# The first chunk of x in two token halves on two queues, all its transposes ahead of the first product

## The chip, the cores and the metric

The kernel runs on one core of one Trainium2 chip. The metric is the device time of one execution in microseconds, from the launch to the end of the last engine; the median of several runs is given. Profiles are of one execution, and their times count from the first instruction that the profiler shows. TensorE (PE in the profile) multiplies, VectorE (DVE), ScalarE (ACT) and GpSimd (POOL) do the elementwise work, and SyncE (SP) mostly starts transfers; ScalarE and GpSimd can start transfers too.

## The reference

One layer of an encoder: a root-mean-square norm of x, one wide input projection, two groups of heads side by side (attention, and a gated linear recurrence, the LRU), and one output projection that is added to x.

```python
def hybrid_layer(x, norm_w, w_in, ...):
    h = rms_norm(x, norm_w)
    proj = jnp.einsum('bsd,de->bse', h, w_in)
    q, k, v, g_attn, xr, g_lru = jnp.split(proj, SPLITS, axis=-1)
    attn_out = attention_group(q, k, v, q_norm_w, k_norm_w)
    lru_out = lru_group(xr, conv_w, conv_b, ...)
    mixed = jnp.concatenate([rms_norm(attn_out, attn_norm_w) * jax.nn.silu(g_attn),
                             rms_norm(lru_out, lru_norm_w) * jax.nn.silu(g_lru)], axis=-1)
    return x + jnp.einsum('bse,ed->bsd', mixed, w_out)
```

x has 512 tokens by 2048 columns, w_in 2048 by 4608, w_out 2048 by 2048, all in float32. Only the start of the input projection matters for this change.

## The kernel before

**The products.** Each float32 operand is split into a high part, rounded to a type that TensorE takes in one pass (`fp32r` in the profile), and the low rest; a product is the sum of three, high by high, high by low and low by high. The first projection is `proj_feat(C_XR, a1, first, given)`: it has the LRU's input features on the partitions and all 512 tokens as the moving operand, four accumulators of 128 by 512 (`pj`), and it walks over the 2048 columns of x in eight chunks of 256 (`c`), each of two halves of 128 (`kk`). For the first two chunks (line 394) the products go in six groups of four per chunk: high weight by high x, low weight by high x, high weight by low x, first for one half, then for the other. Between the groups the generator yields, and the caller does other work there (`move`, lines 1206 to 1221): loads and transposes of later chunks of x, splits of later weights.

**x.** `xload` (line 239) loads one chunk of x as 4 tiles of 128 tokens by 256 columns (`b` in the profile) on SyncE's queue, in `nk` pieces by columns. `xturn` (line 254) turns one half of it so that the columns lie on the partitions: four transposes on TensorE (line 258), one per token tile, into one bank of PSUM. ScalarE then multiplies by the norm's weights and rounds (line 263), which makes the high part, and VectorE makes the low part (line 266). The division by the root mean square comes later, on the results. `columns` (line 190) turns the norm's weights themselves by one small transpose (line 194).

**Weights.** `wraw` (line 205) loads 256 rows by 512 columns of `w_in` on SyncE's queue, here in two pieces of 128 rows, and `wsplit` (line 216) splits one such piece: a copy that rounds (line 223; on VectorE for the first chunk), and a subtraction on VectorE (line 224).

**The start.** TensorE's instructions run in the order of the program text. It begins with `WARM` = 12 fillers (`busy`, line 1165: bf16 products of a tile of ones with itself into a bank that nobody reads), which need the tile `ones` that VectorE writes at line 159. Then come lines 1178 to 1192: the loads are started in the order first half of x's chunk by columns, first weight piece, second half of x, second weight piece, all by SyncE, with the norm's weights by ScalarE. ScalarE loads its function table with a one-column Exp. TensorE turns the norm's weights, turns the first half of x (`xturn(xc, 0, split_first)`, where `split_first` puts the first weight piece's split ahead of x's scaling), and does `WARM2` = 5 more fillers. The first group of four products follows (`proj_feat` then yields `None`), and at line 1224 the second weight piece is split, the second half of x is turned and scaled, and the next chunk's loads are started.

Later chunks of x below `TURNED` = 5 go through `xchunk` and `xturn` too; the last three are turned by VectorE and a trip through device memory instead (`blocks`, `put_aside`, `bring_back`).

Of the kernel before, what the change touches and what calls it, by code (L numbers as in the profile page):

```python
# [17 lines left out]
P = 128  # L18
# [3 lines left out]
NT = SEQ // P  # L22
# [17 lines left out]
SOON = 150  # L40


WARM, WARM2 = 12, 5


BEGIN, STEPS, LATE = 11, 2, 3
# [10 lines left out]
C_Q, C_K, C_GA, C_XR, C_GL = 0, 1024, 1536, 2560, 3584  # L57
# [6 lines left out]
def hybrid_kernel(  # L64
# [20 lines left out]
    nc = tc.nc  # L85
    xf = x.rearrange("b s d -> (b s) d")
# [31 lines left out]
    def nm(s):  # L118
        cnt[0] += 1
        return f"{s}_{cnt[0]}"  # L120

    def x2():
        return pools["xw"].tile([P, SEQ], F32R, tag="x2", bufs=32, name=nm("x2"))
# [4 lines left out]
    def b4(dt=F32, shape=(P, 2, SEQ)):  # L128
        return pools["lru"].tile(list(shape), dt, tag="b4", bufs=LRU_B4, name=nm("b4"))
# [13 lines left out]
    def mm():  # L143
        return ps.tile([P, SEQ], F32, tag="mm", name=nm("mm"))

    def const(shape, name, dt=F32):
        return cp.tile(list(shape), dt, tag=name, name=name)

    def f(ap):
        return ap.bitcast(F32)  # L150
# [7 lines left out]
    ones = const([P, P], "ones")  # L158
# [46 lines left out]
    def wraw(w, r0, c0, nk=1, queue=nc.sync):  # L205

        raw = wring.tile([P, 2, SEQ], F32, name=nm("wr"))
        src = w[r0 : r0 + 2 * P, c0 : c0 + SEQ].rearrange("(k p) e -> p k e", p=P)
        for k in range(nk):
            ks = slice(k * 2 // nk, (k + 1) * 2 // nk)  # L210
            loads_done[queue] = queue.dma_start(raw[:, ks, :], src[:, ks, :]).ins
            yield raw
# [3 lines left out]
    def wsplit(raw, k, copy=nc.scalar.copy):  # L216

        turn_of[0] += k
        pool = pools["wx" if "wx" in pools and turn_of[0] % 2 else "xw"]
        hi = pool.tile([P, SEQ], F32R, tag="wh", bufs=4, name=nm("wh"))  # L220
        lo = pool.tile([P, SEQ], F32R, tag="wl", bufs=4, name=nm("wl"))
        done = (
            copy(hi, raw[:, k, :]).ins,  # L223
            nc.vector.tensor_sub(lo, raw[:, k, :], f(hi)).ins,  # L224
        )
        split_done[-1] = split_done[turn_of[0] - k] = done
        return hi, lo
# [8 lines left out]
    ssq = const([P, NT, KT // 2], "ssq")  # L236
    highs, x_parts, squared = {}, [], []

    def xload(c, nk=1):

        xc = b4(shape=(P, NT, 2 * P))
        for k in range(nk):
            ks = slice(k * 2 * P // nk, (k + 1) * 2 * P // nk)
            cs = slice(c * 2 * P + ks.start, c * 2 * P + ks.stop)
            nc.sync.dma_start(xc[:, :, ks], xf[:, cs].rearrange("(t p) d -> p t d", p=P))
            yield xc

    def behind(those):
        stack = ExitStack()
        for ins in those:  # L250
            stack.enter_context(tc.issue_after(ins))
        return stack

    def xturn(xc, kk, then=None):
        pt = mm()
        for t in range(NT):
            ks = slice(kk % 2 * P, (kk % 2 + 1) * P)
            nc.tensor.transpose(pt[:, t * P : (t + 1) * P], xc[:, t, ks], ident)  # L258
        if then:
            then()  # L260
        xh[kk], xl[kk] = x2(), x2()
        with behind(split_done[-1] if kk > 3 else ()):
            highs[kk // 2] = nc.scalar.activation(
                xh[kk], pt, AF.Identity, scale=nw[:, kk : kk + 1]
            ).ins
        nc.vector.scalar_tensor_tensor(
            xl[kk], pt, nw[:, kk : kk + 1], f(xh[kk]), op0=ALU.mult, op1=ALU.subtract
        )

    def xsquare(xc, c):  # L270
        for t in range(NT):
            if c >= TURNED:
                nc.scalar.activation(
                    xc[:, t, :], xc[:, t, :], AF.Square, accum_out=ssq[:, t, c : c + 1]
                )
                continue
            square = nc.vector.scalar_tensor_tensor(
                xc[:, t, :], xc[:, t, :], 1.0, xc[:, t, :], op0=ALU.mult, op1=ALU.mult,
                accum_out=ssq[:, t, c : c + 1],
            )  # L280
            if c == 1:
                squared.append(square.ins)

    def blocks(u, t, src):

        nc.vector.transpose(
            u[:, :, :, t, :].rearrange("p b k r -> p k b r"),
            src.rearrange("p (k b c) -> p k b c", k=2, c=B),
        )

    def put_aside(u, tag, bufs):

        aside_ = dram.tile([P, NQ, 2 * SEQ // NQ], F32, name=nm(tag), tag=tag, bufs=bufs)
        nc.sync.dma_start(aside_, u.rearrange("p b k t r -> p b (k t r)"))
        return aside_
# [9 lines left out]
    def in_order(v):  # L305
        return v.rearrange("p (t i r) -> p i t r", t=NT, i=NQ)

    def xchunk(c):
        with tc.high_priority(AHEAD):
            (xc,) = xload(c)  # L310
        yield
        if c < TURNED:
            with tc.high_priority(AHEAD):
                for k in range(2):
                    xturn(xc, 2 * c + k)
            if c == 2:
                yield
            with behind(split_done[2][1:] if c == 2 else ()):
                xsquare(xc, c)
            yield  # L320
            return
        u, back = (
            ring.tile([P, NQ, 2, NT, B], F32, name=nm("xu")) for ring in (aring, hring)
        )
        with tc.high_priority(AHEAD), tc.issue_after(squared[-1] if c == TURNED else split_done[3][1]):
            for t in range(NT):
                blocks(u, t, xc[:, t, :])
        yield
        with tc.high_priority(AHEAD):
            there = put_aside(u, "xd", KT // 2 - TURNED)  # L330
        with tc.issue_after(highs[TURNED - 1]):
            xsquare(xc, c)
        yield
        with tc.high_priority(AHEAD):
            bring_back(back, there)
        yield
        with tc.high_priority(AHEAD), behind(split_done[-1]):
            for k in range(2):
                kk = 2 * c + k
                xh[kk], xl[kk] = x2(), x2()  # L340
                hi, lo = (in_order(v) for v in (xh[kk], xl[kk]))
                v = back[:, :, k]
                nc.scalar.activation(v, v, AF.Identity, scale=nw[:, kk : kk + 1])
                x_parts[:] = nc.scalar.copy(hi, v).ins, nc.vector.tensor_sub(lo, v, f(hi)).ins
        yield
# [31 lines left out]
    def xstats():  # L377
        s = const([P, NT], "xsum")
        nc.vector.reduce_sum(s, ssq, axis=AX.X)
        rsqrt_mean(rstd, s, DM, NT)  # L380
        yield from rows(rbc, rstd, lambda: k2(F32R, (P, NT, P)))
# [778 lines left out]
    ctx.enter_context(tc.manual_schedule(engines={mybir.EngineType.PE}))  # L1160

    a1, a2, a3, a4, a5 = [], [], [], [], []
    warm, wv = mm(), ones.bitcast(mybir.dt.bfloat16)

    def busy(n):
        for _ in range(n):
            nc.tensor.matmul(warm[:, : 2 * P], wv[:, :P], wv, start=True, stop=True)  # L1167
# [8 lines left out]
    )  # L1176
    given = {}
    with tc.high_priority():
        xs, ws = xload(0, 2), wraw(w_in, 0, C_XR, 2)
        nc.scalar.dma_start(nw_st, norm_w.rearrange("(k p) -> k p", p=P))  # L1180
        xc, raw = next(xs), next(ws)
        next(xs), next(ws)
        table = const([P, 1], "table")
        nc.scalar.activation(table, ones[:, :1], AF.Exp)
        first = []

        def split_first():
            first.append(wsplit(raw, 0, nc.vector.tensor_copy))

        columns(nw, nw_st)  # L1190
        xturn(xc, 0, split_first)
        busy(WARM2)
    stats = xstats()
    chunks = [xchunk(c) for c in range(1, KT // 2)]

    raws = {}
# [26 lines left out]
    for step in proj_feat(C_XR, a1, first, given):  # L1223
        if step is None:
            with tc.high_priority():
                first.append(wsplit(raw, 1, nc.vector.tensor_copy))
                xturn(xc, 1)
            xsquare(xc, 0)
            move(None)
            given[1] = wload(w_in, 2 * P, C_XR)  # L1230
            continue
        c, e = step
        move(step)
        if (c, e) == (1, 2):
            s2.close()
        if (c, e) == (4, 2):
            with tc.high_priority(AHEAD):
                vec_load()
        if (c, e) == (7, 1):
            columns(vec, vec_st)  # L1240
        if (c, e) in ((4, 3), (KT // 2 - 1, 0)):
            with tc.high_priority(AHEAD), tc.issue_after(split_done[-1][1]):
                next(stats)
# [216 lines left out]
```

## Time and profile before

| what | value |
|---|---|
| median of 3 runs | 626.5 us (626.13, 626.61, 626.5) |
| the profiled execution | 626.48 us, of which its span is 624.7 us |
| TensorE busy | 620.0 us of the span |
| VectorE, ScalarE, GpSimd busy | 495.3, 352.4, 101.8 us |
| x's first two transfers, 256 KB each | 2.9 us from issue to landing |

In the rows below, the first two numbers of the chain and of the timeline are the start and the duration in microseconds, then come the engine, the line, the operation, the tiles written and read, and how many instructions the row merges. A bracket tells how long the engine was idle before and what released it. "PEld" is TensorE's weight load, and "SPq" and "ACTq" mark instructions that only start a transfer. In the chain a row begins where the row before it ended, so its times can differ by some tenths from the timeline's, where pipelined instructions overlap.

### The profile page before, as it was taken

To read this page: it belongs to the slowest core of one execution; us is meant where nothing else is said; L and a number is where in the kernel's file an instruction comes from. 1 tells how busy PE (TensorE), PEld (TensorE's weight loads), DVE (VectorE), ACT (ScalarE), POOL (GpSimd) and SP (SyncE) were. 2 spreads that over 40 slices of the span, in tenths; PEclk is the share of its full clock that TensorE was granted. 3 is DMA by queue.
4 is the path that set the end of the run, shared out by engine and by line. 5 is a ranking of instruction groups with operands and counts; after the bars stand their busy time and mean duration, and the time that the engine had idled before them with its cause. 6 is when DMAs were issued, how large, how long until landed. Compare 5 with 4: busy or idle time off the path is not lost.

```text
span 624.7 us, 8293 instructions
## 1 busy us (share of the span) xinstructions
PE 620.0 (99%) x2756; PEld 512.6 (82%) x2756; DVE 495.3 (79%) x800; ACT 352.4 (56%) x617; POOL 101.8 (16%) x135
## 2 busy tenths in 40 slices
PE   9999999999999999999999999999999999999997
PEld 7888888888888888888888888888888888888886
DVE  5958979986699876887887888549979866887776
ACT  3675799479946833545485548338345633443441
POOL 0000210112003622622123223100210101010010
PEclk9999999999999999999999999999999999999999
DMA  8878686759774599479659646932995777897252
GB/s 285 277 210 271 178 202 171 175 135 195 239 235 137 170 247 240 100 204 270 192 173 258 201 137 192 256 91 76 283 254 184 216 250 242 288 333 230 68 202 101
DMA packets 74026, 127.61 MB, mean 204 GB/s; under 512 B 6664, under 2 KB 29312, under 8 KB 73984
## 3 DMA queue, kind: packets, MB, share of 16 engines
q1 hardware_dynamic: 66096, 109.65, 56.7%
q0 software_dynamic: 7712, 17.31, 14.3%
q8 instruction: 21, 0.34, 0.2%
q14 instruction: 21, 0.17, 0.1%
q10 hardware_dynamic: 176, 0.14, 0.1%
HBM read 110.29 MB, written 37.75 MB: 237 GB/s over the span
## 4 chain that ended last, share of the span: by engine, by line
PE 99%; DVE 0%; issue 0%
PE pj L154 20%; PE pj L155 20%; PE pj L153 20%; PE mm L1040 14%; PE pj L1040 11%; PE mm L155 4%; PE mm L154 3%; PE mm L153 3%; PE pj L394 2%; PE mm L258 1%; PE mm L1167 1%; PE mm L836 0%; DVE cb L1069 0%; PE mm L194 0%; PE mm L373 0%; DVE ones L159 0%
## 5 line engine op out<-in xcount | busy, mean ns | idle before, releaser
L153 PE MATMUL pj<-x,wh 128*128 128x512 f32 x368 | 143.5, 390 | 0.0
L155 PE MATMUL pj<-x,wl 128*128 128x512 f32 x368 | 143.2, 389 | 0.0
L154 PE MATMUL pj<-x,wh 128*128 128x512 f32 x368 | 143.2, 389 | 0.0
L223 ACT CAST wh<-wr 128x512 fp32r<-128x512 f32 x142 | 84.5, 618 | 81.5 <-PE pj L154 29.8
L224 DVE TENSOR_TENSOR wl<-wr,wh 128x512 fp32r<-128x512 f32 x144 | 98.5, 712 | 20.5 <-ACT wh L223 19.2
L888 ACT CAST wh<-wr 128x1024 fp32r<-128x1024 f32 (+1 forms) x72 | 60.6, 860 | 75.3 <-PE mm L1040 36.0
L889 DVE TENSOR_TENSOR wl<-wr,wh 128x1024 fp32r<-128x1024 f32 (+1 forms) x72 | 68.6, 983 | 29.0 <-ACT wh L888 28.9
L153 PEld LDWEIGHTS pj<-x,wh 128*128 128x128 f32 x368 | 69.1, 188 | 14.4
L154 PEld LDWEIGHTS pj<-x,wh 128*128 128x128 f32 x368 | 69.1, 188 | 14.3
L155 PEld LDWEIGHTS pj<-x,wl 128*128 128x128 f32 x368 | 69.1, 188 | 14.3
L154 PE MATMUL pj<-wl,x 128*128 128x512 f32 x192 | 74.7, 389 | 0.0
L155 PE MATMUL pj<-wh,x 128*128 128x512 f32 x192 | 74.7, 389 | 0.0
L153 PE MATMUL pj<-wh,x 128*128 128x512 f32 x192 | 74.7, 389 | 0.0
L912 POOL DMA_DIRECT2D t<-in_w_out_dram x40 | 33.6, 907 | 156.0 <-DMA t<-in_w_out_dram 96.9
L1040 PE MATMUL mm<-wh,ml 128*128 128x512 f32 x126 | 49.0, 389 | 0.0
L1040 PE MATMUL mm<-wh,mh 128*128 128x512 f32 x126 | 49.0, 389 | 0.0
L1040 PE MATMUL mm<-wl,mh 128*128 128x512 f32 x126 | 49.0, 389 | 0.0
L153 PEld LDWEIGHTS pj<-wh,x 128*128 128x128 f32 x192 | 36.0, 188 | 7.6
L154 PEld LDWEIGHTS pj<-wl,x 128*128 128x128 f32 x192 | 36.0, 188 | 7.5
L155 PEld LDWEIGHTS pj<-wh,x 128*128 128x128 f32 x192 | 36.0, 188 | 7.4
L712 POOL TENSOR_SCALAR p<-p,sm 128x512 f32<-128x512 f32 x32 | 24.2, 761 | 89.4 <-DVE sm L711 89.4
L1040 PE MATMUL pj<-wl,mh 128*128 128x512 f32 (+1 forms) x100 | 38.5, 385 | 0.0
(205 smaller groups left out, 1052.9 us busy)
## 6 DMA issues: line engine op xcount, KB each, us to landing
wr<-in_w_in_dram SPq DMA_DIRECT2D x71, 512.0 KB, 5.0
wr<-in_w_out_dram SPq DMA_DIRECT2D x21, 512.0 KB, 5.1
t<-in_w_out_dram POOLq DMA_DIRECT2D x40, 256.0 KB, 7.1
wr<-t SPq DMA_DIRECT2D x40, 256.0 KB, 5.8
pd<-u SPq DMA_DIRECT2D x16, 512.0 KB, 3.0
pt<-pd SPq DMA_DIRECT2D x64, 128.0 KB, 4.1
t<-in_w_out_dram SPq DMA_DIRECT2D x24, 256.0 KB, 5.3
wr<-in_w_out_dram SPq DMA_DIRECT2D x22, 256.0 KB, 4.2
```

The source lines that it names most:

```text
L153: nc.tensor.matmul(acc, lh, rh, start=start, stop=False)
L154: nc.tensor.matmul(acc, lh, rl, start=False, stop=False)
L155: nc.tensor.matmul(acc, ll, rh, start=False, stop=stop)
L223: copy(hi, raw[:, k, :]).ins,
L224: nc.vector.tensor_sub(lo, raw[:, k, :], f(hi)).ins,
L258: nc.tensor.transpose(pt[:, t * P : (t + 1) * P], xc[:, t, ks], ident)
L394: nc.tensor.matmul(acc[e], w[:, e * P : (e + 1) * P], x_[2 * c + k], start=c == k == j == 0, stop=False,)
L712: last_pool[0] = nc.gpsimd.tensor_scalar(p, p, sm, 0.0, op0=ALU.mult, op1=ALU.add).ins
L888: nc.scalar.copy(hi[:, to], b)
L889: nc.vector.tensor_sub(lo[:, to], b, f(hi[:, to]))
L912: nc.gpsimd.dma_start(dst, src, accum_op=ALU.add)
L1040: nc.tensor.matmul(dst[s][:, es], lh[:, ts_], rh[:, es], start=i == ends_[0] and j == 0, stop=i == ends_[1] and j == 2,)
```

## The change

The first chunk of x is still loaded in two pieces, but by tokens: token tiles 0 and 1 by SyncE, token tiles 2 and 3 by ScalarE, each with all 256 columns. So SyncE's order becomes half of x, first weight piece, second weight piece, and ScalarE's the norm's weights, half of x, table load. `xturn` is taken apart into `xturns`, the transposes, and `xscale`, the scaling and the split. Both halves of the chunk's columns, eight transposes, are turned ahead of the first product; the second half's scaling stays where its turn was, at line 1228 of the old text. Between the transposes and the first product one filler is left of five. The fillers multiply a bf16 constant of ones that the framework's preamble writes, in place of the tile `ones`.

```diff
-WARM, WARM2 = 12, 5
+WARM, WARM2 = 12, 1
...
-    def xload(c, nk=1):
+    def xload(c, queues=(nc.sync,)):
         xc = b4(shape=(P, NT, 2 * P))
-        for k in range(nk):
-            ks = slice(k * 2 * P // nk, (k + 1) * 2 * P // nk)
-            cs = slice(c * 2 * P + ks.start, c * 2 * P + ks.stop)
-            nc.sync.dma_start(xc[:, :, ks], xf[:, cs].rearrange("(t p) d -> p t d", p=P))
-            yield xc
+        n = NT // len(queues)
+        src = xf[:, c * 2 * P : (c + 1) * 2 * P].rearrange("(t p) d -> p t d", p=P)
+        for k, queue in enumerate(queues):
+            ts_ = slice(k * n, (k + 1) * n)
+            queue.dma_start(xc[:, ts_], src[:, ts_])
+        return xc
...
-    def xturn(xc, kk, then=None):
+    def xturns(xc, kk):
         pt = mm()
         for t in range(NT):
             ks = slice(kk % 2 * P, (kk % 2 + 1) * P)
             nc.tensor.transpose(pt[:, t * P : (t + 1) * P], xc[:, t, ks], ident)
-        if then:
-            then()
+        return pt
+
+    def xturn(xc, kk):
+        xscale(xturns(xc, kk), kk)
+
+    def xscale(pt, kk):
         xh[kk], xl[kk] = x2(), x2()
...
-    warm, wv = mm(), ones.bitcast(mybir.dt.bfloat16)
+    warm, wv = mm(), nc.const_aps.tensor(1.0, [P, 2 * P], mybir.dt.bfloat16)
...
-        xs, ws = xload(0, 2), wraw(w_in, 0, C_XR, 2)
         nc.scalar.dma_start(nw_st, norm_w.rearrange("(k p) -> k p", p=P))
-        xc, raw = next(xs), next(ws)
-        next(xs), next(ws)
+        xc, ws = xload(0, (nc.sync, nc.scalar)), wraw(w_in, 0, C_XR, 2)
+        raw = next(ws)
+        next(ws)
...
-        def split_first():
-            first.append(wsplit(raw, 0, nc.vector.tensor_copy))
-
         columns(nw, nw_st)
-        xturn(xc, 0, split_first)
+        pts_ = [xturns(xc, k) for k in range(2)]
         busy(WARM2)
+        first.append(wsplit(raw, 0, nc.vector.tensor_copy))
+        xscale(pts_[0], 0)
...
-                xturn(xc, 1)
+                xscale(pts_[1], 1)
```

More of the change, by code (lines that the diff above doesn't have):

```diff
@@ L309, in xchunk @@
         with tc.high_priority(AHEAD):
-            (xc,) = xload(c)
+            xc = xload(c)
         yield
```

## The prediction

> **What bounds the kernel now.** I read the page first (busy shares and the chain that ended last), then the chain for the first 24 us, then the timeline of that stretch, because the diff touches nothing behind it, and last the transfers and the windows there.
>
> ```profile
> PE 620.0 (99%) x2756; PEld 512.6 (82%) x2756; DVE 495.3 (79%) x800; ACT 352.4 (56%) x617; POOL 101.8 (16%) x135
> PE 99%; DVE 0%; issue 0%
> ```
>
> ```profile
> 1.04 2.74 PE mm L1167 x12
> 3.78 0.21 PE mm L194
> 4.00 1.04 PE mm L258 x4
> 5.04 1.07 PE mm L1167 x5
> 6.11 1.22 PE pj L394 x4
> 7.33 0.44 PE mm L258 x4
> 7.77 3.23 PE pj L394 x14
> 10.99 0.87 PE mm L258 x8
> 11.87 4.13 PE pj L394 x18
> ```
>
> TensorE carries 99% of the chain, so the end moves by what TensorE gains before it becomes dense, and by nothing else. It is dense from 6.11 us on: products of 128x512 follow each other every 0.231 us (3.23 us for 14) and transposes of 128x128 every 0.11 us (0.44 us for 4). Up to 6.11 us it does twelve fillers, the norm weights' transpose (L194), four transposes of x's first 128 columns (L258) and five fillers. The same four transposes took 1.04 us at 4.00 us and 0.44 us at 7.33 us, so the clock was slow at first, by a factor of about two. The first four products took 1.22 us instead of 4 x 0.231 = 0.92 us: 0.30 us lost, which is about 1.3 products at half speed, so the clock turned fast near 6.7 us.
>
> ```profile
> 0.31 0.09 POOL L1445 MEMSET const-bfloat16-1.0<- 128x1 bf16 x1
> 0.72 0.45 ACTq L1180 DMA_DIRECT2D nw_st<-in_norm_w_dram  x1
> ...
> 0.72 0.43 SPq L245 DMA_DIRECT2D b<-in_x_dram  x1
> 0.82 0.17 DVE L159 MEMSET ones<- 128x128 f32 x1 [0.82 <-PEq L1445]
> ...
> 1.20 1.28 ACT L1184 ACT_TABLE_LOAD   x1 [1.20 <-PEq L1445]
> 1.21 0.49 SPq L211 DMA_DIRECT2D wr<-in_w_in_dram  x1
> ...
> 1.74 0.43 SPq L245 DMA_DIRECT2D b<-in_x_dram  x1
> ...
> 2.22 0.51 SPq L211 DMA_DIRECT2D wr<-in_w_in_dram  x1
> ...
> 4.99 0.43 DVE L223 CAST wh<-wr 128x512 fp32r<-128x512 f32 x1 [0.78 <-DMA wr<-in_w_in_dram]
> 5.08 0.69 ACT L263 ACTIVATE x<-mm,nw 128x512 fp32r<-128x512 f32 x1 [2.38 <-PE mm L258]
> ...
> 5.82 1.09 PEld L394 LDWEIGHTS pj<-x,wh 128*128 128x128 f32 x4 [0.19 <-ACT x L263]
> ```
>
> The first product is issued at 5.82 us, released by ScalarE's scaled copy of x (5.08 to 5.77 us), itself released by the four transposes that end at 5.04 us. The weight half's rounding ended earlier, at 4.99 + 0.43 = 5.42 us. So the first link is: x's half landed, four slow transposes, one ScalarE pass of 0.69 us; the five fillers (1.07 us) only cover that pass.
>
> **The change, part by part.** *When x lands.* Before, SP issued x's first 128 columns, a weight half, x's other columns, the other weight half. Now SP issues the first two token tiles, then both weight halves, and ScalarE issues the last two token tiles behind the norm weights. The last two tiles go out at 0.72 + 0.45, about 1.2 us, and the table load (1.28 us) slides from 1.20 to about 1.65 us and ends by 2.95 us, with its small activation of 0.2 us behind it. Nothing on ScalarE is needed before 4.8 us, so that issue is free; it would cost its 0.45 us only if x came 1.7 us earlier than I reckon.
>
> ```profile
> b<-in_x_dram SPq DMA_DIRECT2D x2, 256.0 KB, 2.9
> wr<-in_w_in_dram SPq DMA_DIRECT2D x2, 256.0 KB, 4.4
> ```
>
> ```profile
> 1.00:2.00 1.00, 0.96 (x5) 0.71 (x6) 0.00 (x0) 0.80 (x1) 0.89 (x6) 1.00 0.09 24
> 2.00:3.00 1.00, 1.00 (x7) 0.69 (x6) 0.00 (x0) 0.69 (x2) 0.14 (x1) 1.00 0.92 255
> 3.00:4.00 1.00, 1.00 (x6) 0.49 (x5) 0.00 (x0) 0.00 (x0) 0.00 (x0) 1.00 0.88 294
> 4.00:5.00 1.00, 1.00 (x5) 0.92 (x6) 0.18 (x2) 0.00 (x0) 0.00 (x0) 1.00 0.96 301
> ```
>
> Half of x took 2.9 us from issue to landing, so SP's two tiles land near 0.72 + 2.9 = 3.6 us. No row has a large load on ScalarE's queue, so I bound its landing. By the half of x ahead of all others it is 1.2 + 2.9 = 4.1 us; by the weight halves behind others it is 1.2 + 4.4 = 5.6 us. The bytes give a second pair: by the windows' last column, GB/s, the engines had moved 0.28 MB by 3.0, 0.57 MB by 4.0 and 0.87 MB by 5.0 us; all of x is 0.52 MB, reached at 3.85 us if no weights get between, and x with one weight half is 0.79 MB, reached at 4.7 us. Both tiles and first weight half will share the engines; I take **4.2 us**, near the row of the same size, and keep 3.85 and 5.6 us for the range. Rows of x in one transfer become 1 KB instead of 512 B; I count no gain for it, which errs to the slow side.
>
> The Trainium skill, page "DMA: Bandwidth & Descriptors", section "Issuing engines are not separate DMA queues", says that transfers started from several engines run on the same 16 DMA engines and that only issue time is saved. By that rule alone the second queue brings x no bandwidth, and its landing would go by the bytes (3.85 to 4.7 us here), so the sum stands; the windows, with the engines 88 to 96% busy from 2 us on, agree with it.
>
> *TensorE up to the first product.* The fillers read a constant that GpSimd writes at 0.31 us in the preamble, instead of `ones` (0.82 + 0.17 us). TensorE can start at 0.72 to 0.8 us, when the other engines do, not at 1.04 us: the twelve fillers end near 3.5 instead of 3.78 us. The norm weights follow (0.21 us, to 3.7 us), then two transposes on SP's tiles (2 x 0.26 us at the slow rate of 1.04 us for 4, to 4.2 us), then the two on ScalarE's tiles: 4.2 + 0.52 = 4.72 us. ScalarE's pass runs from about 4.76 to 5.45 us. Under it TensorE does the four transposes of the second 128 columns (1.04 us, to 5.76 us) and the one filler left (1.07 / 5 = 0.21 us), to **5.97 us** against 6.11. So the cover that five fillers gave comes from work that was due anyway, and the bound of the first product passes from ScalarE to TensorE by a few tenths. The weight half must be rounded by then: it is second on SP as before, was rounded by 5.42 us, and even 1.21 + 4.4 + 0.43 = 6.04 us would be only 0.07 us late.
>
> *TensorE behind it.* The four transposes at 7.33 us go: **0.44 us** off the dense part. Of the start, 0.14 us earlier lies in the slow clock and is worth half, 0.07 us. The slow share of the first products is 0.30 us; starting the fillers about 0.3 us earlier can bring between nothing and all of that. Would the clock follow them exactly, 0.32 us less of half speed would be 0.16 us; nothing shows that it does, so I take the middle, 0.08 us. Sum: 0.44 + 0.07 + 0.08 = **0.6 us**.
>
> *What is late next.* VectorE's passes keep their order, weight half, low part, x's low part; they were idle-waiting on the second weight half, which now has 256 KB less ahead of it on SP. The next stops are these:
>
> ```profile
> 10.46 1.15 ACT L223 CAST wh<-wr 128x512 fp32r<-128x512 f32 x2 [1.97 <-DMA wr<-in_w_in_dram]
> ...
> 11.52 1.25 ACT L263 ACTIVATE x<-mm,nw 128x512 fp32r<-128x512 f32 x2
> ...
> 16.32 1.43 DVE L286 STREAM_TRANSPOSE xu<-b 128x256 f32<-128x256 f32 x4 [1.22 <-DMA b<-in_x_dram]
> ...
> 18.96 2.49 DVE L224 TENSOR_TENSOR wl<-wr,wh 128x512 fp32r<-128x512 f32 x4
> ```
>
> ```profile
> 20.75 0.23 PE pj L154
> 20.98 0.24 PE pj L155
> ```
>
> The second chunk's weights land at 10.46 us and ScalarE waits for them before it scales that chunk's x: ready at 11.52 + 0.62 = 12.1 us. TensorE wants it after the eight transposes and six products of the first chunk, 11.87 + 6 x 0.23 = 13.2 us. The margin of 1.1 us takes a gain of 0.6 us even if the landing doesn't move. VectorE's low part for the third chunk, behind x's landing at 16.3 us, is ready at 18.96 + 0.62 = 19.6 us and is wanted at 20.98 us: 1.4 us of margin. SP's later loads are issued one slot sooner (x's fourth transfer at 2.2 us rather than 2.78), which can only widen these. No other row of the chain leaves TensorE, so the 0.6 us should reach the end.
>
> The sum is made on the profiled execution, 626.48 us with a span of 624.7 us; the 1.8 us around the span are untouched. It is 0.02 us below the median of the three runs, 626.5 us, so the forecast is 626.48 - 0.6 = **625.9 us**. A difference under 0.2%, 1.25 us, can't be told from no change by a measurement of this kernel.
>
> **The rivals.** *The clock starts over (slower).* The clock turned fast near 6.7 us, 5.66 us after the first filler. Before, nothing but 1.04 us of transposes stood between two runs of fillers. Now 0.21 + 8 x 0.26 = 2.3 us of transposes and one filler stand there, and if ScalarE's half lands after 4.2 us TensorE is quiet for the difference. If the clock's count starts over at 4.2 us, it turns at 9.86 us: products from 5.97 us run at half speed for 3.89 us and lose 1.95 us, which is 1.65 us more than the 0.30 of now; less the 0.51 us won, 1.1 us slower, **627.6 us**. If it starts over only with the first product, the loss is 5.66 / 2 = 2.83 us and the time 626.48 + 2.53 - 0.51 = 628.5 us. It decides against the change if more than about 1 us of slow products is added, that is if the turn comes after 8.2 us. For it: the fillers exist for some reason and four of five go. Against it: before, the clock turned although transposes filled 1.25 us of the time between 3.78 and 5.04 us.
>
> The Trainium skill, page "TensorE: Matmul & The Clock Gate", Part 4 (PE-mode transpose), states that transposes don't count as TensorE activity for that gate; its Part 1 has the gate looking at free-running windows of about 3.4 us. By that rule the quiet would run from 3.5 us to the filler, and a turn before 8.2 us would need a window that the first fillers fill alone. The trace has too few transposes to settle it.
>
> *ScalarE's half is late, or the gain is eaten (no change).* At 4.7 us the product's start becomes 4.7 + 0.52 + 1.04 + 0.21 = 6.47 us, 0.36 us later than now, against 0.44 us won: 626.4 us. At 5.6 us it is 7.37 us, and 1.26 - 0.44 = 0.8 us are lost: 627.3 us. For it: the weight rows at 4.4 us, and three transfers at once. Against it: both queues now begin with x, and only the first weight half can come beside it.
>
> *An earlier clock (faster).* An earlier x alone gives nothing, since in my sum TensorE works without a pause from its first filler to the first product. But if the earlier fillers let the clock turn by about 4.8 us, the second four transposes take 0.44 instead of 1.04 us and the filler some 0.1 us, so that TensorE is done by 5.3 us and the first product waits for ScalarE alone, until 5.5 us: 0.6 us earlier than 6.11, all of it at the fast rate, with the 0.30 us of slow products and the 0.44 us on top. That is 1.35 us, **625.1 us**. Against it: the fillers begin 0.3 us earlier, and the clock would have to turn 1.9 us earlier. For it: the three runs lie 0.5 us apart, which a turn that isn't tied to the program would give.
>
> **How the numbers follow.** Forecast, 625.5 to 626.2 us: 53%. Late half or eaten gain, 626.2 to 627.3 us: 24%. Clock starts over, 627.2 to 628.5 us: 11%. Earlier clock, 624.9 to 625.5 us: 12%. The range leaves out most of the case in which the clock starts over and the lower part of the earlier one: **625.1 to 627.2 us**. Below 626.5 - 1.25 = 625.25 us lies most of the earlier clock's case and nothing else: 10%. Above 627.75 us lies the worse part of the case in which it starts over: 8%. The rest, 82%, is within 0.2%.
>
> **What would show it.** Right: in the chain the row of eight transposes stands ahead of the first products, the products' first row begins near 6.0 us, none of four transposes follows, the second chunk's eight come near 10.4 instead of 10.99 us, and ScalarE's first pass is released by TensorE near 4.8 us. Wrong on x: TensorE idle before L258, released by the transfer, beyond 4.3 us. Wrong on the clock: more than the first two products at over 0.4 us spacing, so that the first row of products grows by whole microseconds. Wrong on the carry: idle time of TensorE before products between 12 and 25 us, released by ScalarE, VectorE or a weight transfer.

## The result and the profile after

The change makes the kernel slower: a median of 628.83 us in six runs (628.06 to 630.57) against 626.25 us of the kernel before, a ratio of 1.0046 with a 95% interval of 1.0033 to 1.0058. In a later experiment (e14) the same text gave 628.82 us beside 626.27 us. The profiled execution took 628.06 us, the fastest of the six, and its span is 626.2 us, 1.5 us more than before. The forecast was 625.9 us.

On the page TensorE is as busy as before, and a hundredth of the chain has passed to transfers:

```profile
PE 620.5 (99%) x2752; PEld 512.9 (82%) x2752; DVE 495.0 (79%) x800; ACT 352.5 (56%) x617; POOL 101.7 (16%) x135
...
PE 99%; DMA 1%; ACTq 0%; DVE 0%; issue 0%
```

The chain of the changed kernel for its first microseconds (start, duration, what; the lines 258, 263, 394 and 1167 are now L259, L268, L399 and L1172):

```profile
0.72 0.45 ACTq L1184
1.17 0.03 issue
1.20 4.43 DMA b<-in_x_dram
5.64 0.04 issue
5.68 1.54 PE mm L259 x6
7.22 0.21 PE mm L1172
7.44 5.04 PE pj L399 x18
12.47 0.87 PE mm L259 x8
13.35 4.13 PE pj L399 x18
```

The chain no longer begins on TensorE. It goes through ScalarE's issue of the norm weights, the transfer of x's second token half (4.43 us), six transposes and the filler, and reaches the first product at 7.44 us, where it began at 6.11 us before. Three differences give the whole span of this execution:

- the first product begins 7.44 - 6.11 = 1.33 us later;
- the first 18 products take 5.04 us where the next 18 take 4.13 us: 0.91 us lost to the slow clock, where before 0.30 us was lost: 0.61 us more;
- the four transposes behind the first products are gone: 0.44 us less.

1.33 + 0.61 - 0.44 = 1.50 us, against 1.5 us between the spans. The median of the runs lies another 0.8 us higher; e14's profile, below, shows a typical execution. The six transposes at 5.68 us still ran at the slow rate (1.54 us, 0.26 us each), so the slow clock has a part in the first difference too. Behind 12.47 us the rows are the same as before, 0.87 and 4.13 us. The timeline shows who waited:

```profile
0.76 2.72 PE L1172 MATMUL mm<-const-bfloat16-1.0 128*128 128x256 bf16 x12 [0.76 <-PEq L1449]
...
4.05 0.69 PE L259 MATMUL mm<-ident,b 128*128 128x128 f32 x2
...
5.15 0.43 DVE L223 CAST wh<-wr 128x512 fp32r<-128x512 f32 x1 [1.04 <-DMA wr<-in_w_in_dram]
...
5.68 1.54 PE L259 MATMUL mm<-ident,b 128*128 128x128 f32 x6 [0.94 <-DMA b<-in_x_dram]
6.41 0.69 ACT L268 ACTIVATE x<-mm,nw 128x512 fp32r<-128x512 f32 x1 [3.20 <-PE mm L259]
```

Two transposes ran at 4.05 us on SyncE's token tiles. Then TensorE stood for 0.94 us until ScalarE's tiles landed. Each bank of PSUM takes columns from all four token tiles, so ScalarE's pass, which needs a whole bank, was released at 6.41 instead of 5.08 us. The weight had been there since 5.15 us.

### The profile page after: what moved, and what is told of

It is laid out like the page before. It is cut to its first block, busy times and chain, and to the rows that moved or that the text cites. A ratio compares the mean times of both kernels' runs of the same rounds, so it can differ in the third digit from the quotient of the medians.

```text
span 626.2 us, 8284 instructions
## 1 busy us (share of the span) xinstructions
PE 620.5 (99%) x2752; PEld 512.9 (82%) x2752; DVE 495.0 (79%) x800; ACT 352.5 (56%) x617; POOL 101.7 (16%) x135
## 4 chain that ended last, share of the span: by engine, by line
PE 99%; DMA 1%; ACTq 0%; DVE 0%; issue 0%
PE pj L153 20%; PE pj L154 20%; PE pj L155 20%; PE mm L1045 14%; PE pj L1045 11%; PE mm L155 3%; PE mm L154 3%; PE mm L153 3%; PE pj L399 2%; PE mm L259 1%; DMA b<-in_x_dram 1%; PE mm L841 0%; ACTq L1184 0%; DVE cb L1074 0%; PE mm L378 0%; PE mm L1172 0%
## 5 line engine op out<-in xcount | busy, mean ns | idle before, releaser
L1045 PE MATMUL pj<-wh,mh 128*128 128x512 f32 (+1 forms) x100 | 38.5, 385 | 0.0
```

Of the source, the lines that this page charges most:

```text
L1045: nc.tensor.matmul(dst[s][:, es], lh[:, ts_], rh[:, es], start=i == ends_[0] and j == 0, stop=i == ends_[1] and j == 2,)
```

## The experiments

The theory after this profile: the half that ScalarE starts lands late and holds up the first product, and the pause that it makes lets the clock turn late, by an amount that differs from run to run. The rivals: the four fillers that were taken away, the new constant, transposes that don't keep the clock up, the second queue by itself. In each table row, "before" was run beside the kernel on the same chip.

| run | median, us (lowest to highest, runs) | before, us | ratio (95% interval) |
|---|---|---|---|
| e1_both_sp | 628.65 (628.14 to 629.35, 5) | 626.35 | 1.0038 (1.0026 to 1.0050) |
| e2_x_first_on_act | 627.65 (625.99 to 628.11, 10) | 626.35 | 1.0018 (1.0009 to 1.0027) |
| e3_20_fillers | 627.61 (627.07 to 630.04, 10) | 626.35 | 1.0025 (1.0016 to 1.0034) |
| e4_before_1_filler | 626.43 (625.78 to 628.34, 12) | 626.35 | 1.0009 (1.0000 to 1.0018) |
| e5_before_const_13 | 626.17 (625.86 to 626.53, 11) | 626.34 | 0.9998 (0.9989 to 1.0007) |
| e6_pause_filled | 628.28 (626.86 to 630.67, 10) | 626.34 | 1.0037 (1.0024 to 1.0051) |
| e7_turns_as_fillers | 626.48 (626.12 to 626.86, 11) | 626.34 | 1.0001 (0.9992 to 1.0009) |
| e8_weight_third | 627.53 (626.82 to 627.82, 11) | 626.34 | 1.0015 (1.0006 to 1.0023) |
| e9_weight_on_act | 628.9 (627.04 to 629.12, 5) | 626.41 | 1.0033 (1.0020 to 1.0045) |
| e10_columns_weight_on_act | 626.19 (625.68 to 627.88, 11) | 626.41 | 1.0001 (0.9992 to 1.0010) |
| e11_before_4_fillers | 627.38 (626.36 to 627.78, 11) | 626.41 | 1.0013 (1.0004 to 1.0022) |
| e12_columns | 627.38 (625.74 to 627.89, 11) | 626.27 | 1.0010 (1.0000 to 1.0019) |
| e13_columns_filled | 626.03 (625.73 to 626.41, 11) | 626.27 | 0.9995 (0.9986 to 1.0004) |
| e14_changed_again | 628.82 (628.65 to 628.98, 5) | 626.27 | 1.0041 (1.0028 to 1.0053) |

### Which piece lands last: e1, e2, e9

e1 takes the second queue away:

```diff
-        xc, ws = xload(0, (nc.sync, nc.scalar)), wraw(w_in, 0, C_XR, 2)
+        xc, ws = xload(0, (nc.sync, nc.sync)), wraw(w_in, 0, C_XR, 2)
```

> The changed kernel with both token halves of x's first chunk started by SyncE. Theory (the half started by ScalarE lands 1.3 us late, and the pause of TensorE that it makes lets the clock turn fast later): the second half lands at 4.3 to 4.9 us instead of 5.6, the first product begins near 6.2 us instead of 7.4, the pause shrinks from 0.94 to under 0.6 us, and the time falls from 628.8 to 626.0 to 627.0 us. Rival (four fillers fewer, and transposes that don't keep the clock up, cost the time whatever the queue): 628 us or more, with slow products until after 9 us.

The chain of e1:

```profile
1.71 4.73 DMA wr<-in_w_in_dram
6.44 0.02 issue
6.46 0.44 DVE wh L223
6.90 0.14 issue
7.04 6.68 PE pj L399 x18
```

x came earlier, ScalarE's pass was released at 5.28 us, and it helped nothing: now the weight piece was third in SyncE's queue and landed at 6.44 us, and the first product began at 7.04 us, not 6.2. The theory's time was missed by 1.65 us; so was its picture of one late half. What came lies in the rival's range, slow products included: 18 products took 6.68 us where the full rate needs 4.13. Of the rival's two reasons, the transposes are tested in e7 and the missing fillers in e4 and e13. e2 put ScalarE's half of x ahead of the norm weights, which went to SyncE's queue:

```diff
-        nc.scalar.dma_start(nw_st, norm_w.rearrange("(k p) -> k p", p=P))
         xc, ws = xload(0, (nc.sync, nc.scalar)), wraw(w_in, 0, C_XR, 2)
+        nc.sync.dma_start(nw_st, norm_w.rearrange("(k p) -> k p", p=P))
```

> The changed kernel with ScalarE starting its half of x as its first transfer, and the norm weights started by SyncE between its half of x and the weights. Theory (the half is late because it is the second transfer of ScalarE's queue and behind two others in the issue): issued at 0.72 us it lands near 3.6 to 4.2 us, TensorE hardly pauses, and the time is 625.6 to 626.5 us. Rival (a large transfer on ScalarE's queue is slow by itself when SyncE's queue is busy): it lands 4.4 us after its issue, at 5.1 us, and the time is 627.5 us or more.

All packets of ScalarE's half had been moved by 4.0 us, and the eight transposes ran from 4.65 us without a wait, so a large transfer on ScalarE's queue isn't slow in itself. But the 8 KB of norm weights came late:

```profile
4.47 0.25 PE L194 MATMUL mm<-ident,nw_st 16*128 16x16 f32 x1 [0.99 <-DMA nw_st<-in_norm_w_dram]
```

The weight piece was rounded only at 6.10 us, and the first product began at 6.67 us. The time, 627.65 us, lies in the rival's range, but not for the rival's reason. e9 put the first weight piece, instead of a half of x, on ScalarE's queue, with 14 fillers:

```diff
-WARM, WARM2 = 12, 1
+WARM, WARM2 = 14, 1
...
-        xc, ws = xload(0, (nc.sync, nc.scalar)), wraw(w_in, 0, C_XR, 2)
+        xc, ws = xload(0, (nc.sync, nc.sync)), wraw(w_in, 0, C_XR, 2, (nc.scalar, nc.sync))
...
```

> The changed kernel with the second queue given to the first weight piece: SyncE starts both token halves of x, ScalarE the first weight piece behind the norm weights; 14 fillers at the start. x is whole at 4.5 us as with SyncE alone, all eight transposes end near 5.9 us. Theory (the product needs three pieces, and the last of them lands at 5.6 to 6.4 us on whatever queue): the weight lands then, its rounding ends at 6.1 to 6.8 us, the first product begins 0.2 to 0.9 us later than before, less 0.44 us for the transposes: 626.1 to 627.0 us. Rival (it was the second queue alone that made the changed kernel late, by what was put on it): the weight lands at 5.0 us, 625.7 to 626.1 us, faster than before.

```profile
5.83 1.54 PE L260 MATMUL mm<-ident,b 128*128 128x128 f32 x6 [0.86 <-DMA b<-in_x_dram]
```

The weight landed at 5.6 us as expected, but the second half of x, second on SyncE, landed at 5.79 us and not at 4.5, so TensorE waited for x again and the time was 628.9 us: outside the theory's range and the rival's. The three runs together: the last of the three pieces was there at 5.8 to 6.4 us on whichever queue it stood, and a shuffle of the queues only chose who was last.

In the changed kernel itself the queues can be told apart. These are the packets, the MB and the share of the engines' time of SyncE's queue (q1) and ScalarE's (q10) in its profile up to 4.0 us:

```profile
q1 hardware_dynamic: 365, 0.45, 44.1%
q10 hardware_dynamic: 56, 0.03, 2.6%
```

Of ScalarE's packets 32 are the norm weights, so 24 of the 272 of its half of x had been moved, although it was issued at 1.20 us, when SyncE issued its weight piece (1.21 us). The rest went between 4.0 and 5.3 us, and the landing was seen at 5.64 us. So SyncE's half of x and most of its weight piece went ahead of ScalarE's half, not beside it.

### A third piece ahead of the first product, by itself: e8

The kernel before, loads in the order x, x, weight, weight, all on SyncE by columns, and 8 fillers behind the transposes:

```diff
-WARM, WARM2 = 12, 5
+WARM, WARM2 = 12, 8
...
-        xc, raw = next(xs), next(ws)
-        next(xs), next(ws)
+        xc = next(xs)
+        next(xs)
+        raw = next(ws)
+        next(ws)
```

> The kernel before with the loads in the order of the change, whole x first, then the weight, all on SyncE and still in halves by columns, and eight fillers instead of five so that TensorE stays busy; transposes stay where they were. Theory (the first product has to wait for three pieces of 256 KB instead of two): the weight piece lands at 5.8 to 6.3 us instead of 5.0, the first product begins near 6.7 us, time 626.8 to 627.4 us with a small spread. Rival (the order of the pieces is free, the second queue alone makes the product late): 626.2 us plus at most 0.3 for fillers that stand in the way.

Its chain:

```profile
1.75 5.17 DMA wr<-in_w_in_dram
6.91 0.02 issue
6.93 0.44 DVE wh L223
7.37 0.14 issue
7.51 1.16 PE pj L394 x4
```

The weight landed at 6.91 us, 0.6 us later than expected, the first product began at 7.51 us, behind a pause of 1.44 us, and the time rose by 1.2 us, 0.1 us over the range given, with a spread of 1.0 us. This is the price of the order of the loads with nothing else changed but three more fillers.

### The cut by tokens: e10, e12, e14

e10 is e9 with x cut by columns and 13 fillers; e12 is the changed kernel with that cut alone undone, one half on each queue; e14 is the changed kernel again. The edit of e12:

```diff
-        xc, ws = xload(0, (nc.sync, nc.scalar)), wraw(w_in, 0, C_XR, 2)
+        xc, ws = b4(shape=(P, NT, 2 * P)), wraw(w_in, 0, C_XR, 2)
+        for k, queue in enumerate((nc.sync, nc.scalar)):
+            queue.dma_start(xc[:, :, k * P : (k + 1) * P],
+                            xf[:, k * P : (k + 1) * P].rearrange("(t p) d -> p t d", p=P))
```

> The same with x in halves by columns as before, both on SyncE, the first weight piece on ScalarE, 13 fillers: the first four transposes need the first piece alone, at 3.6 us, and ScalarE's pass is done by 5.8 us. Theory (three pieces): bound by the weight piece, first product at 6.1 to 6.8 us, 626.1 to 627.0 us, the same as with token halves, so that the cut by tokens matters little. Rival (the cut by tokens costs the time): 0.5 us or more faster than the kernel with token halves.

> The changed kernel with one thing undone: the two halves of x's first chunk are cut by columns, as before, not by tokens; still one on SyncE and one on ScalarE, eight transposes ahead, one filler, the new constant. Theory (the cut by tokens puts the landing of the later half ahead of the transposes and ScalarE's pass, 1.5 us, instead of beside them): ScalarE's first pass is released near 5.0 us by the first half, the later half still lands near 5.6 us, the first product begins near 6.5 us instead of 7.2, and the time is 626.0 to 627.2 us instead of 628.8. Rival (what costs is the second queue, or the eight transposes ahead of the product, however x is cut): 628.3 us or more.

> The changed kernel as it is, on the same chip as the two others, as their measure: 628.0 to 629.3 us, ScalarE's half landing at 5.5 to 6.4 us, first product at 7.0 to 7.7 us.

Rows of e12's timeline:

```profile
3.68 1.11 PE L259 MATMUL mm<-ident,b 128*128 128x128 f32 x4
...
4.83 0.69 ACT L268 ACTIVATE x<-mm,nw 128x512 fp32r<-128x512 f32 x1 [1.59 <-PE mm L259]
...
5.47 1.12 PE L259 MATMUL mm<-ident,b 128*128 128x128 f32 x4 [0.68 <-DMA b<-in_x_dram]
```

With columns the first four transposes need the first piece alone, and ScalarE's pass runs from 4.83 to 5.52 us, beside the later landing instead of behind it. The first product began at 6.80 us in e12's chain (6.46 us by its issue), as expected. With the queues of e9, the cut (and one filler fewer) is worth 628.9 against 626.19 us, which bears out e10's rival: the time lies in the theory's range too, but the theory had it equal to e9's; with the queues of the change the cut alone is worth 628.82 against 627.38 us, and e12's median is 0.2 us above the range given. e14 came out as expected, its half of x at 6.11 us and its first product at 7.37 us. e12's eleven runs fall in two groups, five from 625.74 to 626.46 us and six from 627.38 to 627.89 us, with none between.

### The clock: e3, e4, e6, e7, e11, e13

e4 and e11 take fillers from the kernel before, e3 adds fillers at the start of the changed kernel, and e6 adds them between its second and third transpose:

```diff
-WARM, WARM2 = 12, 5
+WARM, WARM2 = 12, 1     (e4)
+WARM, WARM2 = 4, 5      (e11)
...
-WARM, WARM2 = 12, 1
+WARM, WARM2 = 20, 1     (e3)
...
             nc.tensor.transpose(pt[:, t * P : (t + 1) * P], xc[:, t, ks], ident)
+            if (kk, t) == (0, 1):     (e6)
+                busy(5)
```

e7 puts transposes (ten and five) in the place of all fillers of the kernel before:

```diff
-WARM, WARM2 = 12, 5
+WARM, WARM2 = 10, 5
...
-            nc.tensor.matmul(warm[:, : 2 * P], wv[:, :P], wv, start=True, stop=True)
+            nc.tensor.transpose(warm[:, :P], ones, ident)
```

> The kernel before with transposes of the 128x128 identity in the place of its fillers: ten at the start, from when the identity is written (1.4 us) to 3.6 us, and five behind x's transposes. TensorE is as busy as before and the first product stays at 5.8 us. If transposes don't count for the clock, the count begins with the first product: slow products until 8 to 11 us, 627.3 to 629 us. If they count as fillers do: 626.2 to 626.7 us.

e7 gave 626.48 us, within the spread of the kernel before. From its chain:

```profile
6.18 1.35 PE pj L394 x4
7.53 0.44 PE mm L258 x4
```

Its first filler began at 1.45 us, and still the first four products took only 1.35 us (1.22 before) and the transposes behind them ran at the full rate: here float32 transposes bring the clock up as well as fillers do.

> The kernel before with one filler instead of five between the transposes and the first product; its loads and transposes stay. TensorE then pauses about 0.8 us under ScalarE's pass, and the first product stays at 5.8 us. Theory (pauses put the turn of the clock off): some runs turn later, time 626.3 to 627.5 us with a wider spread than 0.6 us. Rival (the fillers removed have nothing to do with it): 626.2 us as before.

> The kernel before with 4 fillers at the start instead of 12: they end near 1.9 us and TensorE pauses until the norm weights at about 2.8 us and x at 3.7 us. The first product stays at 5.8 us. Theory (a pause puts the clock's turn off by up to its own length and more): slow products until 6 to 9 us, 626.8 to 627.8 us with a spread over 1 us. Rival (only what stands directly ahead of the products counts): 626.3 us as before.

e4 takes away the same four fillers as the change. It left the loads alone and only let TensorE stand 0.67 us ahead of the first product. Six of its twelve runs stayed at 625.78 to 626.15 us; the other six lay at 626.72 to 628.34 us. The profiled one was of the first kind: its fillers, begun at 1.04 us, had the clock up by the first transposes (0.60 us for four). e11, with a pause of 1.23 us at 2.1 us and full cover behind, lay between 626.36 and 627.78 us; its first four products took 1.79 us instead of 0.92:

```profile
3.73 1.12 PE mm L258 x4
4.85 1.07 PE mm L1167 x5
5.92 1.79 PE pj L394 x4
7.70 0.85 PE mm L258 x4
```

> The changed kernel with 20 fillers at the start instead of 12, which end near 5.0 us, so that the norm weights and the first two transposes run just before ScalarE's half lands; the landing and the first product stay where they are (5.6 and 7.4 us). Theory (of the 2.6 us lost, 0.9 us is the later start of the products and the rest is the clock, which turns later because TensorE pauses): products at full rate from the first on, time 626.7 to 627.3 us, and the spread of the runs falls from 2.5 us to under 0.6. Rival (the clock doesn't depend on that pause): no change, 628.8 us with the same spread.

> The changed kernel with five more fillers in the place of its pause, between the second and the third transpose, while TensorE waits for ScalarE's half of x. Nothing else moves; the first product stays near 7.2 us. Theory (part of the loss is a clock that turns late because TensorE does no products or fillers from 3.3 to 7.1 us): 627.0 to 627.9 us instead of 628.8. Rival (the clock is not concerned): 628.8 us with the same spread.

e3 has the late first product (7.33 us) and still a pause of 1.00 us, but its 18 products took 4.42 us in the profiled execution; eight of ten runs lay between 627.07 and 627.89 us, the other two at 628.87 and 630.04 us. The median is 0.3 us above the theory's range and the spread, 3.0 us, is not the 0.6 expected. So some 1.2 us of the changed kernel's loss remain without most of the clock's share, as in e8, and the median fell by 1.2 us. e6 says less: its half of x landed at 6.36 us, TensorE stood 0.81 us behind the new fillers, and the ten runs spread from 626.86 to 630.67 us. Its median of 628.28 us lies between the theory's range and the rival's value.

What can follow a pause is seen best in e14's profile, in the windows (stretch, its length, the busy time of PE, PEld, DVE, ACT and POOL with their instructions in brackets, then PEclk, the granted clock, the share of the transfer engines and GB/s):

```profile
6.00:7.00 1.00, 0.85 (x7) 0.71 (x7) 0.16 (x1) 0.37 (x1) 0.00 (x0) 1.00 1.11 389
7.00:7.80 0.80, 0.57 (x4) 0.38 (x3) 0.45 (x1) 0.80 (x2) 0.00 (x0) 1.00 1.06 387
8.00:9.00 1.00, 1.00 (x4) 0.81 (x3) 0.97 (x3) 0.00 (x0) 0.00 (x0) 0.50 1.07 369
9.00:10.00 1.00, 1.00 (x4) 0.81 (x3) 1.00 (x3) 0.92 (x2) 0.00 (x0) 0.50 1.09 349
10.00:11.00 1.00, 1.00 (x4) 0.71 (x4) 1.00 (x7) 0.22 (x1) 0.00 (x0) 0.50 1.09 347
11.00:12.00 1.00, 1.00 (x5) 0.87 (x4) 1.00 (x4) 0.00 (x0) 0.00 (x0) 0.86 1.09 372
```

in its timeline, and in the row of its chain that holds the first 18 products:

```profile
3.91 0.69 PE L259 MATMUL mm<-ident,b 128*128 128x128 f32 x2 [0.16 <-DMA b<-in_x_dram]
6.15 0.88 PE L259 MATMUL mm<-ident,b 128*128 128x128 f32 x6 [1.55 <-DMA b<-in_x_dram]
6.87 0.27 PE L1172 MATMUL mm<-const-bfloat16-1.0 128*128 128x256 bf16 x1
7.37 1.68 PE L399 MATMUL pj<-x,wh 128*128 128x512 f32 x4 [0.23 <-ACT x L268]
8.85 1.91 PE L399 MATMUL pj<-x,wl 128*128 128x512 f32 x4
10.56 1.66 PE L399 MATMUL pj<-x,wh 128*128 128x512 f32 x5
...
7.37 5.98 PE pj L399 x18
```

Here the fillers had brought the clock up in time: six transposes took 0.88 us. Then the granted clock fell to 0.50, in the middle of dense products, four to a microsecond. It was whole up to 7.8 us, half from 8 to 11 us, and 0.86 in the last window is 0.28 us of half speed: so from about 7.9 to 11.3 us. TensorE had stood for 1.55 us before 6.15 us. Four products from 8.85 to 10.56 us are 0.43 us each where the rate is 0.23. So a pause can cost twice over: it is lost itself, and it can be paid again later, after the work has resumed.

The sum of the result holds for this execution too: 1.26 us later start, 5.98 - 4.13 = 1.85 us lost to the slow clock where 0.30 was (1.55 us more), 0.44 us of transposes gone, together 2.37 us, against 627.1 - 624.7 = 2.4 us. The granted clock doesn't show every slow stretch: it reads 1.00 at 4 to 5 us of the kernel before, where four transposes took 1.04 instead of 0.44 us, so a slow start is read from the spacing of the instructions alone. The mean granted clock was 0.996 or 0.997 in all five runs of e14, which is what some 3.4 us at half speed make of 627 us, and 0.999 or 1.000 in the six of the result. There no such fall is on record; its profile shows a clock that turned late.

> The same with five fillers between the first four and the second four transposes, and 13 instead of 12 at the start, so that TensorE hardly pauses. Theory (a pause of TensorE ahead of the products makes the clock turn late in some runs): the first product stays near 6.5 us, no run above 627 us, median 625.9 to 626.4 us. Rival (the fillers only stand in the way): 0.3 us or more slower than the kernel without them.

```diff
-WARM, WARM2 = 12, 1
+WARM, WARM2 = 13, 1
...
-        pts_ = [xturns(xc, k) for k in range(2)]
+        pts_ = [xturns(xc, 0)]
+        busy(5)
+        pts_.append(xturns(xc, 1))
```

e13 is e12 with these fillers, and so removes both causes, the cut and most of the pause (0.34 us is left). Its chain:

```profile
1.20 4.50 DMA b<-in_x_dram
5.70 0.04 issue
5.75 0.66 PE mm L259 x4
6.41 0.11 PE mm L1172
6.51 4.13 PE pj L399 x18
```

All 18 products run at the full rate (4.13 us), no run lies above 626.41 us, against 627.38 us for the median of e12, and the group of e12 at 627.4 to 627.9 us is gone. e13's profiled span is explained as the changed kernel's was: 0.40 us later start, 0.30 us of slow products gone, 0.44 us of transposes gone: -0.34 us, against 624.4 - 624.7 = -0.3 us. Its median is 0.24 us under that of the kernel before, which the interval doesn't tell from no change.

### The fillers' constant: e5

```diff
-WARM, WARM2 = 12, 5
+WARM, WARM2 = 13, 5
...
-    warm, wv = mm(), ones.bitcast(mybir.dt.bfloat16)
+    warm, wv = mm(), nc.const_aps.tensor(1.0, [P, 2 * P], mybir.dt.bfloat16)
```

> The kernel before with one part of the change alone: the fillers read the preamble's constant and so start at 0.76 instead of 1.04 us, with 13 of them so that they end where twelve did. Theory (the fillers hold the clock's count, and the change's loss lies in the loads): a little earlier turn of the clock, first product unmoved at 5.8 us, 626.0 to 626.3 us. Rival (fillers on that constant don't work as fillers): 627 us or more with a wide spread, as in the changed kernel.

626.17 against 626.34 us, no difference that can be measured; the constant is harmless, and the earlier start brings nothing that shows. The profile shows where it went in this execution:

```profile
12.95 1.20 PE L394 MATMUL pj<-x,wh 128*128 128x512 f32 x4 [0.49 <-ACT x L263]
```

The clock was up by x's transposes (0.66 us for four) and the first product was issued at 5.28 us instead of 5.82, but the second chunk's weights landed at 11.15 us where they had at 10.46, TensorE waited for what ScalarE makes behind them, and at 16 us it was level with the kernel before (15.98 against 16.00 us).

## Why the prediction was wrong

**What bounds the kernel** was right: the end moved by what happened on TensorE ahead of its dense part, and the sum of three terms (start, slow products, transposes) gives the spans of the changed kernel and of e13 to a tenth of a microsecond. It does as well for e1, e2, e3, e6, e9 and e14; for e12 and e10 it is 0.2 and 0.3 us off, for a reason that is open.

**The landing of ScalarE's half** is the step that failed. "I take 4.2 us", with bounds of 3.85 and 5.6 us; it was 5.64 us in the first profile and 6.11 us in e14, over the upper bound, and the first product came at 7.44 us instead of 5.97. The value came from the row of x's half that stood ahead of all other traffic, though this half was the third large piece to be started along with the weight. The row of the weight halves, at the other end, was nearer. Against a late half the prediction put that "both queues now begin with x, and only the first weight half can come beside it"; the packets show that the weight came ahead of it: by 4.0 us SyncE's queue had moved 0.45 MB, more than its half of x, and ScalarE's 0.03 MB. The rule cited there (the Trainium skill, page "DMA: Bandwidth & Descriptors", section "Issuing engines are not separate DMA queues") agrees with the runs: by 5.0 us the engines had moved 0.87 MB in e1, from one queue, and 0.83 MB in the changed kernel, from two. It would have moved the estimate to the 4.7 us that the prediction worked out from the bytes, still 0.9 us short. In e1, e2 and e9 the last of three pieces of 256 KB was there at 5.8 us at the earliest, and at 5.43 us in e12, while the change makes the first product wait for three where two were enough.

**"TensorE works without a pause from its first filler to the first product"** followed from that value and fell with it: 0.94 us of pause, 1.55 us in e14. The sum had put the pause and any added slow products at nothing; the slow products alone added 0.61 us in the first profile and 1.55 us in e14. The price of the second four transposes was right (0.44 us). But the working knew that ScalarE's pass waits for the third and fourth token tile, and took that landing for early enough not to matter: with the cut by tokens the later landing stands ahead of the pass, with the cut by columns beside it, and e10 and e12 show what that is worth.

**The rivals** were the right ones, taken apart wrongly. The late half was priced at 627.3 us for a landing at 5.6 us, with a first product at 7.37 us; it came at 7.44 us. The clock that starts over was priced at 627.6 us upward. They were given chances as if one excluded the other, but the late half, with four of five fillers gone, makes the pause that makes the clock late, so they came together: 627.3 us and 1.5 us more. Eight chances in a hundred for "slower" were far too few for that reason.

**The clock's rule.** The Trainium skill, page "TensorE: Matmul & The Clock Gate", Part 4 (PE-mode transpose), by which transposes don't count as activity, was cited for that rival. The trace disagrees: e7, with transposes for all its fillers, took 626.48 us beside 626.34 us. What e4, e11 and e12 have in common is that TensorE stands; in e13, where fillers cover most of that, no run lies above 626.41 us. Part 1's window of about 3.4 us agrees with e14, where the clock was granted at half from about 7.9 to 11.3 us.

**Right**: the fillers' earlier start (0.76 us), the free issue on ScalarE. The margins behind 12 us were not tested by the change, which came to them 1.5 us later than before; in e5's profile, with an earlier start, the margin of the second chunk's weights was used up and 0.49 us more.

What stays open: why the engines took SyncE's pieces ahead of ScalarE's, and what passes between the last packet (5.3 us in the first profile, some 5.55 us in e14) and the landing (5.64 and 6.11 us). Open too is how much standing the clock allows: the profiles of e4 and e12 show pauses of 0.7 us, and about half of their runs were slower by 0.7 to 2.3 us than the others; no run measured the limit.

## What to carry to other kernels

Ahead of a dense engine, count the transfers that must all have landed before its first instruction, and give each the landing of its place in the whole traffic, not the landing that a first transfer has on its queue. Cut a load so that the first piece alone feeds a whole step of the chain: a cut across the step makes the last piece's landing come before the step instead of beside it. And where a clock follows activity, price a pause twice and look at the spread of the runs, not at one profile: with one filler instead of five (e4), half of the runs looked unharmed.

## What was not expected of the hardware

The granted clock can fall after the pause is over, in the middle of dense work: 0.50 from about 7.9 us in e14, though TensorE had resumed at 6.15 us after standing 1.55 us. Executions of one text differ in this: the changed kernel's runs lay between 628.06 and 630.57 us. And moving 8 KB of norm weights from the head of one queue to the second place of another (e2) held TensorE for 0.99 us.
